# The output projection of a two-branch decoder layer: 512 columns of weights per matmul in place of 256, products in another order

## The chip, the cores and the metric

The kernel runs on one core of a Trainium2 chip. The metric is the device time of one execution in microseconds; the number quoted for a kernel is the median of several runs. The profile is one execution, recorded instruction by instruction, and its span is the time from the first to the last instruction.

## The reference

The layer computes, for a sequence of 512 rows and a model width of 1024 in fp32:

```python
h = rms_norm(x, norm_w)
proj = h @ w_in                       # all queries, keys, values and gates at once
y_a = moba(...) * silu(z_a)           # block-sparse attention, 8 heads
y_b = nsa(...) * silu(z_b)            # compressed + selected + window attention, 8 heads
merged = sigmoid(g_a) * (y_a @ w_branch_a) + sigmoid(g_b) * (y_b @ w_branch_b)
out = x + merged @ w_out              # [512 x 1024] @ [1024 x 1024]
```

The change touches the last line alone: the product with `w_out` and the addition of `x`.

## The kernel before, in words

All large products are made in split precision. An fp32 operand becomes a rounded high part and a remainder, and `mm3` (L373 to L387) multiplies with three matmuls: high by high, low by high, high by low. The stationary operand of the output projection is a 128x128 piece of `merged` (tiles `m`, `mh`, `ml`), and the moving operand is a row of weights.

The product with `w_out` is made from seven half-size products in place of eight. The two matrices are cut into quarters; sums of quarters are multiplied, and the results are added to or taken from the quarters of the output. The sums of `merged` are made by `m_sums` (L1600) on VectorE and ScalarE while the stage before it ends. The sums of weights are made in DRAM by `sum_weights` (L565), which copies one quarter into the buffer `wsum` and adds another quarter by a DMA that accumulates; the GpSimd queue issues the last of these at 406.16 us. `operand(p_, w, j)` (L559) says which DRAM piece product `p_` reads: 1, 2 and 4 read plain quarters of `w_out`, 5, 6, 3 and 7 read sums.

The weights come through one stream, `W` (L316 to L371), a list of tiles in the order of their use. A tile of 128x512 fp32 (256 KB) is loaded by the SP queue into one of six raw buffers (`wr`, L328). Then ScalarE or GpSimd rounds it (`wh`, L350 and L354) and VectorE takes the remainder (`wl`, L359), after which the raw buffer is free for the tile six places on. There are eight buffers for `wh` and eight for `wl`. `W.split` is called to keep the conversion up to four tiles ahead of the matmuls.

The whole program is written out by a planner: it keeps an estimated clock for each engine, and an instruction goes into an engine's stream when the estimate lets it start. Each engine then runs its stream strictly in order, and semaphores hold an instruction until its inputs are there. So a wait in the streams of VectorE, ScalarE or SP also holds all that is queued behind it.

`last` (L1619) writes the output projection. Before the change it works on 256 columns at a time. A tile of weights holds two of the four 128-row slices of a quarter, each 256 columns wide. The order is product 1 and then product 2 for both column halves, then products 5, 6, 3, 7, 4 for the first half, then the same five for the second. For each product and half, two blocks of 128 output rows (`t` is 0 and 1) are made one after the other, each by 12 matmuls of 256 columns into one PSUM bank. After each of these 28 results, `add` (L1638) lets VectorE add a quarter of it, with its sign, to the residual tile `xr` (L1641). The matmuls of a later product go on into the same PSUM accumulator, so they wait for the add before them. When an output block of 128x256 is complete, the SP queue stores it. The four tiles of `x` for the right half (`xr`, 128x512 each) are loaded at the start of `last`, on the same SP queue.

In all the stage issues 7 products x 2 halves x 2 blocks x 4 slices x 3 = 336 matmuls of 256 columns, with 28 weight tiles. The stage before it makes the gated merge (`pbr` and `pgw` are its PSUM tiles), and its last matmul is followed at once by the first of `last`.

## Time and profile before

| what | value |
|---|---|
| three runs | 458.43, 459.62, 459.7 us; median 459.62 us |
| span of the profiled execution | 458.3 us; its own time is not listed apart, the shortest run is 0.1 us above the span |
| TensorE busy (PE) | 450.0 us, 98% of the span |
| VectorE, ScalarE, GpSimd busy | 382.1, 299.7 and 203.8 us |
| first matmul of the output projection | 413.07 us |
| its last matmul starts | 454.51 us |
| last instruction of VectorE starts | 454.83 us |

PE is the matmul part of TensorE and PEld its load of the stationary operand, which runs beside the matmuls. In the trace a matmul is shown from its start until its result is out, and the next one starts before that; so the time that one costs in a stream is the distance from start to start, and not the duration in the row. SPq is the DMA queue of SyncE.

### The profile page before, as it was taken

The page shows a single profiled execution, that of the slowest core. Times are in us where ns is not written, and L with a number is a line of the kernel's source. Part 1 is how long each engine was busy: PE and PEld are TensorE (multiplying, and loading weights), DVE is VectorE, ACT ScalarE, POOL GpSimd, SP SyncE. Part 2 cuts the span into 40 slices and gives each one's busy share as a digit, 9 for nine tenths or more (in the row PEclk, how much of TensorE's full clock was granted, in tenths as well). Part 3 has the DMA queues.
Part 4 walks back from the last instruction along what each step waited for, and adds up shares of the span by engine and source line. Part 5 has one row for each costly group of instructions (what it writes and reads, how often), then busy time and mean ns, then how long its engine had stood idle before and what let it go on. Part 6 is the DMA issues. An engine that isn't in the chain of part 4 may idle for free.

```text
span 458.3 us, 8879 instructions
## 1 busy us (share of the span) xinstructions
PE 450.0 (98%) x2935; PEld 406.5 (89%) x2935; DVE 382.1 (83%) x951; ACT 299.7 (65%) x705; POOL 203.8 (44%) x243
## 2 busy tenths in 40 slices
PE   9999999999999999999999999999999999999996
PEld 7888888899778898889999999989988999999996
DVE  6987799889997787878899899878957699898862
ACT  6865668767978797467786777669654256445420
POOL 1263337865774572276776454655741211210020
PEclk9999999999999999999999999999999999999999
DMA  8876646887965869769978967975866888878862
GB/s 275 280 249 208 210 141 211 195 231 189 261 180 159 226 212 281 249 150 271 250 188 205 243 152 189 272 170 123 254 158 180 238 235 249 233 217 309 263 198 69
DMA packets 55230, 98.23 MB, mean 214 GB/s; under 512 B 5328, under 2 KB 10064, under 8 KB 55184
## 3 DMA queue, kind: packets, MB, share of 16 engines
q1 hardware_dynamic: 39952, 68.30, 46.5%
q0 software_dynamic: 7616, 14.68, 19.6%
q10 hardware_dynamic: 7616, 14.68, 9.5%
q8 instruction: 23, 0.38, 0.3%
q14 instruction: 23, 0.19, 0.1%
HBM read 90.69 MB, written 36.31 MB: 277 GB/s over the span
## 4 chain that ended last, share of the span: by engine, by line
PE 73%; DVE 13%; DMA 5%; ACT 5%; issue 3%; SPq 0%; POOL 0%; DVEq 0%; ACTq 0%; POOLq 0%
PE pgw L384 17%; PE pgt L384 14%; PE pbr L384 10%; PE pgc L384 7%; PE pgf L652 5%; PE O L1082 5%; PE pt L1048 4%; PE po L384 4%; PE sps L1001 2%; PE sps L1002 2%; DVE wl L359 2%; DMA wr<-wsum 2%; DMA T<-rtab 1%; DMA wr<-in_w 1%; DVE sb L1020 1%
## 5 line engine op out<-in xcount | busy, mean ns | idle before, releaser
L359 DVE TENSOR_TENSOR wl<-wr,wh 128x512 fp32r<-128x512 f32 (+1 forms) x150 | 102.6, 696 | 4.7 <-ACT wh L350 2.8
L350 ACT CAST wh<-wr 128x512 fp32r<-128x512 f32 (+1 forms) x125 | 74.1, 608 | 19.3 <-DMA wr<-wsum 11.3
L354 POOL TENSOR_SCALAR wh<-wr 128x512 fp32r<-128x512 f32 (+1 forms) x44 | 33.4, 770 | 115.6 <-DVE wl L359 30.6
L1039 POOL TENSOR_SCALAR P<-P,sst,gate 128x512 f32<-128x512 f32 (+3 forms) x56 | 46.5, 832 | 40.0 <-DVE sst L1038 30.1
L1035 ACT ACTIVATE P<-sb,sst 128x512 f32<-128x512 f32 (+3 forms) x88 | 50.7, 577 | 17.4 <-DVE sst L1020 16.1
L1020 DVE CUSTOM_DVE_ANT_0 sb<-sps,T 128x512 f32<-128x512 f32 (+3 forms) x96 | 45.9, 482 | 15.4 <-PE sps L1002 13.3
L384 PE MATMUL pgt<-wl,hh 128*128 128x512 f32 (+2 forms) x160 | 56.2, 351 | 0.8 <-DVE wl L359 0.8
L384 PE MATMUL pgt<-wh,hh 128*128 128x512 f32 (+2 forms) x160 | 56.9, 355 | 0.0
L384 PE MATMUL pgt<-wh,hl 128*128 128x512 f32 (+2 forms) x160 | 56.2, 351 | 0.0
L384 PE MATMUL pgw<-th,wh 128*128 128x256 f32 x240 | 50.4, 285 | 0.3 <-DVE gm L1493 0.3
L1060 ACT CAST ph<-pt 128x512 fp32r<-128x512 f32 (+2 forms) x72 | 33.8, 476 | 20.8 <-PE pt L1048 19.6
L384 PE MATMUL pgw<-hh,wh 128*128 128x256 f32 x160 | 45.7, 285 | 0.1
L384 PE MATMUL pgw<-hh,wl 128*128 128x256 f32 x160 | 45.0, 281 | 0.0
L384 PE MATMUL pgw<-hl,wh 128*128 128x256 f32 x160 | 44.8, 280 | 0.0
L384 PEld LDWEIGHTS pgw<-th,wh 128*128 128x128 f32 x240 | 40.0, 190 | 1.0 <-DVE gm L1493 0.7
L1048 PE MATMUL pt<-cst,P 128*128 128x128 f32 x232 | 40.7, 273 | 0.2 <-DVE pl L1062 0.2
L1062 DVE TENSOR_TENSOR pl<-pt,ph 128x512 fp32r<-128x512 f32 (+2 forms) x72 | 38.7, 548 | 1.8 <-ACT ph L1060 1.6
L427 POOL TENSOR_TENSOR nr<-nss,mhalf 128x8 f32<-128x8 f32 (+1 forms) x16 | 27.2, 1697 | 21.2 <-DVE nss L426 17.8
L384 PEld LDWEIGHTS pgt<-wl,hh 128*128 128x128 f32 x160 | 30.0, 188 | 5.5 <-DVE wl L359 1.2
L384 PE MATMUL pgw<-th,wl 128*128 128x256 f32 x120 | 33.9, 282 | 0.0
L384 PEld LDWEIGHTS pgt<-wh,hh 128*128 128x128 f32 x160 | 30.1, 188 | 3.8 <-ACT nraw L695 0.2
L384 PEld LDWEIGHTS pgt<-wh,hl 128*128 128x128 f32 x160 | 30.1, 188 | 3.7
(267 smaller groups left out, 1346.1 us busy)
## 6 DMA issues: line engine op xcount, KB each, us to landing
wr<-wsum SPq DMA_DIRECT2D x56, 256.0 KB, 4.3
wr<-in_wtok SPq DMA_DIRECT2D x36, 256.0 KB, 4.5
wsum<-in_wgate ACTq DMA_DIRECT2D x16, 512.0 KB, 4.9
wsum<-wsum POOLq DMA_DIRECT2D x14, 512.0 KB, 6.9
wr<-in_wgate SPq DMA_DIRECT2D x24, 256.0 KB, 4.7
xsum<-th SPq DMA_DIRECT2D x16, 256.0 KB, 2.1
T<-rtab SPq DMA_DIRECT2D x16, 256.0 KB, 5.3
wr<-in_w SPq DMA_DIRECT2D x16, 256.0 KB, 4.3
```

What stands on the lines that cost most here:

```text
L350: e.copy(hi, raw)
L354: e.tensor_scalar(hi, raw, 1.0, 1.0, op0=ALU.mult, op1=ALU.mult)
L359: c.do({"D": cd(n)} if lead else either(n), lambda e, hi=hi, lo=lo, raw=raw: e.tensor_sub(lo, raw, hi.bitcast(F32))).mark((w, 1, i))
L384: nc.tensor.matmul(dst, sts[i][a], mvs[i][b], start=(start and i == a == b == 0), stop=(stop and i == n - 1 and b == 1), skip_group_check= ...
L427: c.do({"p": 430 + POWC * w}, lambda e: e.tensor_tensor(v(dst), v(ss), mhalf[:parts, :w], op=ALU.pow))
L652: nc.tensor.matmul(ps[t][:, :n], (hl if a else hh)[:, k, t * P:(t + 1) * P], w[b], start=(k == a == b == 0), stop=(k == KT - 1 and b == 1))
L1020: e.tensor_tensor_reduce(z["sb"][:, :L], sps[:, :L], T[:, S - L:], scale=-1.0, scalar=3e38, op0=ALU.add, op1=ALU.min, accum_out=st[:, 0, b ...
L1035: e.activation(pv(), z["sb"][:, :L], AF.Exp, bias=st[:, 0, b:b + 1], scale=-1.0, accum_out=st[:, 1, b:b + 1])
L1039: c.do({"P": 315 + 0.834 * L}, lambda e: e.tensor_scalar(pv(), pv(), st[:, 2, b:b + 1], g, op0=ALU.mult, op1=ALU.mult))
L1048: nc.tensor.transpose(pt[:, (b - kb) * P:(b - kb + 1) * P], u.p0 if u.p0 is not None and b == 0 else u.pb[:, POFF[b] + kb * P:POFF[b] + (k ...
L1060: e.copy(z["w"][0], pt[:, :w])
L1062: ch.do({"D": cd(w)}, lambda e: e.tensor_sub(z["w"][1], pt[:, :w], z["w"][0].bitcast(F32)), pt)
```

## The change

The stage keeps its seven products, its 28 tiles of weights and its three matmuls per slice, but:

- A tile of weights holds one 128-row slice of a quarter, 512 columns wide (the host's layout `wo` changes, and with it what lies in the four tiles of each sum).
- A matmul streams 512 columns. For each slice the three matmuls are made for block 0 and then for block 1, each in its own PSUM bank, so a tile serves 6 matmuls of 512 columns where it served 12 of 256.
- The products come in the order 1, 2, 6, 5, 7, 3, 4, each for all columns.
- Product 4, the last, is made slice by slice for block 0 at full width, then for block 1 in two column halves (24 matmuls of 256 columns), the second half in a fresh PSUM bank. The part of product 7 that the second half needs is added by an extra VectorE instruction.
- The adds are 128x512, with three of 128x256 at the end, 16 in place of 28. The stores are seven of 128x512 and two of 128x256 in place of 16 of 128x256.
- The loads of `x` for the right half stand between the slices of product 2 in place of the start of `last`.

So 13 groups of 12 matmuls of 512 columns (156) and 24 matmuls of 256 columns take the place of 336.

The core of the diff:

```diff
@@ -590,8 +590,8 @@
         for p_ in (5, 6, 3, 7):
             tiles.append((operand(p_, 1, j), 512))
         tiles += [(wbr[j, 1], 512), (operand(4, 1, j), 512), (wbr[j + 4, 1], 512)]
-    for p_, c in [(p_, c) for p_ in (1, 2) for c in range(2)] + [(p_, c) for c in range(2) for p_ in (5, 6, 3, 7, 4)]:
-        tiles += [(operand(p_, 2, 2 * c + i), 512) for i in range(2)]
+    for p_ in (1, 2, 6, 5, 7, 3, 4):
+        tiles += [(operand(p_, 2, k), 512) for k in range(4)]
     from_att = set()
     for n_ in ORDER_T:
         if n_ in tlay and tlay[n_][1] == KT:
@@ -1617,10 +1617,6 @@
             mt[n_ + 1, k] = hi, lo, (c, d)[n_ // 2], 256 * (n_ % 2)
 
     def last(ms, xr):
-        for t in range(NT):
-            xr[t, 1] = att("xr", F32)
-            dma(xr[t, 1], x[t * P:(t + 1) * P, 512:], 2048)
-
         def st(p_, t):
             if p_ in (1, 2, 3):
                 r, k0 = {1: (0, 0), 2: (0, 4), 3: (2, 4)}[p_]
@@ -1633,33 +1629,55 @@
                 r.append((hi[:, z], lo[:, z], ch))
             return r
         ps, rd = {}, {}
-        tags = {("a", 0): "ss", ("a", 1): "tt", ("b", 0): "to", ("c", 0): "to", ("b", 1): "gg", ("c", 1): "gg"}
-
-        def add(c, z_, t, r, half, end=False, free=False):
-            xv = xr[r, half][:, c * 256:(c + 1) * 256]
-            src = ps[z_, c, t]
-            ch = Chain(now[0] + 230).do({"D": 335}, lambda e: e.scalar_tensor_tensor(
-                xv, src[:, :256], -0.25 if half else 0.25, xv, op0=ALU.mult, op1=ALU.add), src if free else None)
+        tags = {"a": "ss", "c": "tt", "b": "to"}
+        H = slice(0, 256), slice(256, 512)
+
+        def add(z_, t, r, half, end, free, z):
+            xv, n = xr[r, half][:, z], z.stop - z.start
+            src = ps[z_, t]
+            ch = Chain(now[0] + 230).do({"D": cd(n)}, lambda e: e.scalar_tensor_tensor(
+                xv, src[:, z], -0.25 if half else 0.25, xv, op0=ALU.mult, op1=ALU.add), src if free else None)
             if end:
-                ch.call(lambda: dma(out[r * P:(r + 1) * P, (c + 2 * half) * 256:(c + 2 * half + 1) * 256], xv, 1024))
+                ch.call(lambda: dma(out[r * P:(r + 1) * P, 512 * half + z.start:512 * half + z.stop], xv, 4 * n))
             return ch
-        rest = ((5, "b", True), (6, "a", False), (3, "b", False), (7, "a", False), (4, "a", False))
-        for c, p_, z_, first in ([(c, *z) for z in ((1, "a", True), (2, "c", True)) for c in range(2)] +
-                                 [(c, *z) for c in range(2) for z in rest]):
-            ws = W.take(2, 256)
-            for t in range(2):
-                if first:
-                    tag = tags[z_, c][t]
-                    yield room(tag)
-                    ps[z_, c, t] = psum(tag, "po")
-                elif (z_, c, t) in rd:
-                    yield rd[z_, c, t].ready
-                yield from mm3(ps[z_, c, t][:, :256], st(p_, t), ws, start=first, again=not first)
-                W.split(W.i + 4 + 2 * t)
-                r, half, end, free = {1: (t, 0, False, False), 5: (t + 2, 1, False, False), 6: (t + 2, 0, False, False),
-                                      3: (t + 2, 0, True, True), 7: (t + 2, 1, True, False), 2: (t, 0, True, True),
-                                      4: (t, 1, True, True)}[p_]
-                rd[z_, c, t] = add(c, z_, t, r, half, end, free)
+        def out_of(p_, t):
+            return {1: (t, 0, False, False), 5: (t + 2, 1, False, False), 6: (t + 2, 0, False, False), 3: (t + 2, 0, True, True),
+                    7: (t + 2, 1, True, False), 2: (t, 0, True, True), 4: (t, 1, True, True)}[p_]
+
+        def part(dst, p_, t, k, w, z, start, again):
+            yield from mm3(dst[:, z], [st(p_, t)[k]], [(w[0][:, z], w[1][:, z], w[2])], start=start and not k, stop=(k == 3),
+                           again=again)
+            W.split(W.i + 4)
+
+        full = slice(0, 512)
+        for p_, z_, first in ((1, "a", True), (2, "c", True), (6, "a", False), (5, "b", True), (7, "a", False), (3, "b", False)):
+            for k in range(4):
+                if p_ == 2:
+                    xr[k, 1] = att("xr", F32)
+                    dma(xr[k, 1], x[k * P:(k + 1) * P, 512:], 2048)
+                w = W.take(1, 512)[0]
+                for t in range(2):
+                    if not k:
+                        if first:
+                            yield room(tags[z_][t])
+                            ps[z_, t] = psum(tags[z_][t], "po")
+                        else:
+                            yield rd[z_, t].ready
+                    yield from part(ps[z_, t], p_, t, k, w, full, first, not first)
+                    if k == 3:
+                        rd[z_, t] = add(z_, t, *out_of(p_, t), full)
+                        if (p_, t) == (7, 1):
+                            add(z_, t, t, 1, False, False, H[1])
+        ws = W.take(4, 512)
+        for t, z_, z in ((0, "a", full), (1, "a", H[0]), (1, "d", H[1])):
+            if z_ == "d":
+                yield room("g")
+                ps[z_, t] = psum("g", "po")
+            else:
+                yield rd[z_, t].ready
+            for k in range(4):
+                yield from part(ps[z_, t], 4, t, k, ws[k], z, z_ == "d", z_ == "a")
+            add(z_, t, *out_of(4, t), z)
 
     def cmp():
         yield from compress_h(0)
@@ -1753,7 +1771,7 @@
     w2 = np.stack([f[k][0].reshape(2, P, DH).transpose(1, 0, 2) for k in ("cmp_w2_k", "cmp_w2_v")], 1)
     wbr = np.stack([np.concatenate([ch(f[k][0][:, j * P:(j + 1) * P]) for k in ("w_branch_a", "w_branch_b")], 0)
                     for j in range(8)])
-    wo = f["w_out"][0].reshape(2, 2, 2, P, 2, 2, 256).transpose(4, 0, 5, 1, 3, 2, 6).reshape(4, 4, P, 512)
+    wo = f["w_out"][0].reshape(2, 4, P, 2, 512).transpose(3, 0, 1, 2, 4).reshape(4, 4, P, 512)
     onehot, cd = _consts()
     cd.update(pos=posT.reshape(P, -1), w2=w2.reshape(P, -1))
     d = dict(x=f["x"][0], xT=f["x"][0].T[P:],
```

The planner's streams are the same up to the stage's start; from there they move. The first place is the SP queue behind the loads of the sixth and seventh weight tile of the stage (`wr_6001`, `wr_6014`; the tiles are counted from 0). `wr` are raw weight tiles, `xr` the residual, `wsum` the buffer of summed weights. Before:

```order
L253 DMA wr_6001<-in_wout 128x512
L253 DMA wr_6014<-in_wout 128x512
L253 DMA xr_6030<-in_x 128x512
L253 DMA xr_6032<-in_x 128x512
L253 DMA xr_6034<-in_x 128x512
L253 DMA xr_6036<-in_x 128x512
L253 DMA wr_6064<-wsum_151 128x512
L253 DMA wr_6089<-wsum_151 128x512
L253 DMA wr_6135<-wsum_151 128x512
L253 DMA wr_6164<-wsum_151 128x512
L253 DMA out_y<-xr_5991 128x256 x2
```

The same place after the change:

```order
L253 DMA wr_6001<-in_wout 128x512
L253 DMA wr_6014<-in_wout 128x512
L253 DMA wr_6048<-wsum_151 128x512
L253 DMA wr_6063<-wsum_151 128x512
L253 DMA wr_6071<-wsum_151 128x512
L253 DMA xr_6087<-in_x 128x512
L253 DMA xr_6104<-in_x 128x512
L253 DMA xr_6118<-in_x 128x512
L253 DMA wr_6122<-wsum_151 128x512
L253 DMA wr_6128<-wsum_151 128x512
L253 DMA wr_6137<-wsum_151 128x512
```

The first three loads of summed weights (tiles 8, 9 and 10) moved ahead of the loads of `x`; before, all four loads of `x` stood ahead of tile 8.

The second place is VectorE during the first two products. `gm`, `ma`, `mb`, `ml` belong to the merge and its sums, `wl` is the remainder of a weight tile, and `xr<-po` is an add. Before:

```order
L1573 TENSOR_TENSOR gm_4686<-gm_4686,gm_5813 128x512
L1641 SCALAR_TENSOR_TENSOR xr_5991<-po_6038,xr_5991 128x256
L359 TENSOR_TENSOR wl_6056<-wr_5943,wh_6055 128x512
L1329 TENSOR_TENSOR ma_6024<-gm_4685 128x256
L1641 SCALAR_TENSOR_TENSOR xr_5991<-po_6059,xr_5991 128x256
L1577 TENSOR_TENSOR ml_6023<-gm_4686,mh_6022 128x512
L1330 TENSOR_TENSOR ma_6024<-gm_4686,ma_6024 128x256
L1641 SCALAR_TENSOR_TENSOR xr_5991<-po_6084,xr_5991 128x256
L1332 TENSOR_TENSOR mb_6025<-gm_4686,gm_4685 128x256
L1344 TENSOR_TENSOR ml_6027<-ma_6024,mh_6026 128x256
L359 TENSOR_TENSOR wl_6058<-wr_5965,wh_6057 128x512
L1333 TENSOR_TENSOR mb_6025<-ma_6024,gm_4686 128x256
```

After (the row `gm_4686` stands ahead of these too, and `wl_6037`, `wl_6052` are tiles 4 and 5, `wl_6067` is tile 6):

```order
L359 TENSOR_TENSOR wl_6037<-wr_5943,wh_6036 128x512
L359 TENSOR_TENSOR wl_6052<-wr_5965,wh_6051 128x512
L1329 TENSOR_TENSOR ma_6024<-gm_4685 128x256
L1577 TENSOR_TENSOR ml_6023<-gm_4686,mh_6022 128x512
L1330 TENSOR_TENSOR ma_6024<-gm_4686,ma_6024 128x256
L1332 TENSOR_TENSOR mb_6025<-gm_4686,gm_4685 128x256
L1638 SCALAR_TENSOR_TENSOR xr_5991<-po_6030,xr_5991 128x512
L1333 TENSOR_TENSOR mb_6025<-ma_6024,gm_4686 128x256
L1638 SCALAR_TENSOR_TENSOR xr_5991<-po_6038,xr_5991 128x512
L1341 SCALAR_TENSOR_TENSOR ml_6027<-ma_6024,mh_6026 128x256
L1344 TENSOR_TENSOR ml_6029<-mb_6025,mh_6028 128x512
L359 TENSOR_TENSOR wl_6067<-wr_6001,wh_6066 128x512
```

The remainders of tiles 4 and 5 moved ahead of the merge's sums. Two adds of 512 columns stand where four of 256 stood, and the remainder of tile 6 stands behind both of them and behind the last of the sums. One piece of the sums (`ml_6027<-ma_6024,mh_6026`, 128x256) moved from VectorE to GpSimd, ahead of the rounding of tile 6 (`wh_6066`). That is the only rounding left to GpSimd in the stage; it had six there, and ScalarE does the other five now.

## The prediction

> **What bounds the kernel now.** I read the page first: its span, the busy time of the engines, the clock, and the chain that ended last.
>
> ```profile
> span 458.3 us, 8879 instructions
> PE 450.0 (98%) x2935; PEld 406.5 (89%) x2935; DVE 382.1 (83%) x951; ACT 299.7 (65%) x705; POOL 203.8 (44%) x243
> PEclk9999999999999999999999999999999999999999
> PE 73%; DVE 13%; DMA 5%; ACT 5%; issue 3%; SPq 0%; POOL 0%; DVEq 0%; ACTq 0%; POOLq 0%
> ```
>
> TensorE sets the time, at its full clock from end to end. The stage at issue is the last, so what it saves on TensorE should come off the end one for one, if its supply holds. Next the instructions of the tile `po` by shape, in one view:
>
> ```profile
> L384 PE MATMUL po<-wh,mh x88: 278/283/355, 413.8 to 454.3; 128*128 128x256 f32 x88
> L384 PE MATMUL po<-wh,ml x88: 279/283/283, 413.9 to 454.4; 128*128 128x256 f32 x88
> L384 PE MATMUL po<-wl,mh x88: 279/283/387, 414.0 to 454.5; 128*128 128x256 f32 x88
> L384 PE MATMUL po<-wh,m x48: 278/283/283, 413.1 to 447.9; 128*128 128x256 f32 x48
> L384 PE MATMUL po<-wl,m x24: 283/283/283, 413.3 to 448.0; 128*128 128x256 f32 x24
> ```
>
> These are 88+88+88+48+24 = 336 matmuls. Their 283 ns are not what one costs, since they overlap; the distance between starts is, and the timeline of PE gives it. Its rows for the stage's start, its two breaks and its end (start, duration, what):
>
> ```profile
> 413.07 0.40 PE L384 MATMUL po<-wh,m 128*128 128x256 f32 x2
> ...
> 422.55 0.28 PE L384 MATMUL po<-wh,ml 128*128 128x256 f32 x1
> 422.99 0.39 PE L384 MATMUL po<-wl,mh 128*128 128x256 f32 x1 [0.16 <-DVE wl L359]
> 423.21 0.28 PE L384 MATMUL po<-wh,mh 128*128 128x256 f32 x1
> ...
> 436.41 0.28 PE L384 MATMUL po<-wl,mh 128*128 128x256 f32 x1
> 437.29 0.35 PE L384 MATMUL po<-wh,mh 128*128 128x256 f32 x1 [0.61 <-DVE xr L1641]
> 437.49 0.28 PE L384 MATMUL po<-wh,ml 128*128 128x256 f32 x1
> ...
> 453.31 0.28 PE L384 MATMUL po<-wh,ml 128*128 128x256 f32 x1
> ...
> 454.51 0.28 PE L384 MATMUL po<-wl,mh 128*128 128x256 f32 x1
> ```
>
> From 453.31 to 454.51 lie ten distances: 0.120 us each. At that pace 335 distances make 40.20 us; from 413.07 to 454.51 it took 41.44. The missing 1.24 us are the two breaks: 0.44 and 0.22 where 0.12 each was due (0.42 lost), 0.88 and 0.20 (0.84 lost), 1.26 together. So the stage costs 336 x 0.120 + 1.26 = 41.58 us, nearly all of it matmuls one behind the other.
>
> **The change: the matmuls.** Removed are 336 x 0.120 = 40.32 us. Added are 156 matmuls of 512 columns and 24 of 256. No `po` row has 512 columns, so I look for the nearest rows on PE that do:
>
> ```profile
> 7.62 1.09 PE L652 MATMUL pgf<-wl,hh 128*128 128x512 f32 x4
> ...
> 16.95 1.09 PE L652 MATMUL pgf<-wh,hh 128*128 128x512 f32 x4
> ...
> 410.33 0.40 PE L384 MATMUL pbr<-yh,wh 128*128 128x512 f32 x1
> ```
>
> The first product of the kernel (`pgf`) goes from 7.62 to 16.95 in ten groups of four: 9.33/40 = 0.2333 us. The twelve `pbr` just ahead of the stage go from 410.33 to 413.07: 0.2283. I take 0.2333: there, as in the new stage, the weights are streamed and the PSUM bank changes between matmuls. In `pbr` the weights stand still and one bank is filled. The new stage is then 156 x 0.2333 + 24 x 0.120 = 36.39 + 2.88 = 39.27 us, a gain of 1.05 us on the matmuls (1.83 with the pace of `pbr`; none if 512 columns cost 2 x 0.120). A tile of weights now serves 6 x 0.2333 = 1.40 us.
>
> A rule speaks for less. The Trainium skill, TensorE: Matmul & The Clock Gate, section Wait — 56ns, not 53.3ns?, gives a warm matmul a fixed part of only about 2.5 ns beside its columns. By that, 156 fixed parts fewer would be an estimate of 0.39 us in place of 1.05. The rows here disagree: two halves cost 240 ns and the whole 228 to 233, so a fixed part of 7 to 12 ns goes with each.
>
> **The breaks.** Both are late weights. The first, 422.55, is the remainder of a tile of sums. The chain of waits and the list of DMA issues tell the second, and why loads were slow (first row: start, length; others: count, size, median us from issue to landing; then the total wait of the SP queue, times, longest):
>
> ```profile
> 429.18 6.12 DMA wr<-wsum
> ...
> wr<-wsum SPq DMA_DIRECT2D x56, 256.0 KB, 4.3
> xr<-in_x SPq DMA_DIRECT2D x8, 256.0 KB, 8.2
> out_y<-xr SPq DMA_DIRECT2D x16, 128.0 KB, 2.2
> SPq L253 <- DVE xr L1641: 19.9, 15, 6.4
> ```
>
> A load took 6.12 us from 429.18, and its tile stopped PE at 436.41. The loads of `x` took twice as long as a tile's, and in the SP queue the stage's stores waited 19.9 us for adds, each holding the loads behind it. What the change does to this, from the SP queue's own timeline before:
>
> ```profile
> 408.31 2.50 SPq L253 DMA_DIRECT2D wr<-in_wout  x2
> 410.90 4.05 SPq L253 DMA_DIRECT2D xr<-in_x  x4
> 415.45 4.38 SPq L253 DMA_DIRECT2D wr<-wsum  x4
> ```
>
> Tile 8, the first of sums, was issued at 415.45 behind four loads of `x`. Its raw buffer is free once VectorE has taken the remainder of tile 2, which ran at 411.31 (row below), so now it goes at about 412.0, 3.4 us sooner. Two stores (product 2) stand among the loads of tiles where ten did; the others follow the last tile. They wait for adds that PE lets start near 423.8 and 424.5, and hold the load of tile 16 to about 425.6. Needed is tile 16 at 413.07 + 16 x 1.40 = 435.5, less 1.3 us to round it and take its remainder: 8.6 us for a landing that took 4.3 in the median. So neither break should come back. I count 1.26 us gained, with 0 as the other end.
>
> **VectorE.** It sums less: 28 adds become 13 wide and 3 narrow. What counts is the queue in front of tile 6, where the merge's sums and two wide adds stand. Its rows (timeline, then groups of the last stage with count, busy us and mean ns):
>
> ```profile
> 411.31 0.68 DVE L359 TENSOR_TENSOR wl<-wr,wh 128x512 fp32r<-128x512 f32 x1
> 414.55 0.68 DVE L1573 TENSOR_TENSOR gm<-gm,gm 128x512 f32<-128x512 f32 x1
> 418.78 0.68 DVE L359 TENSOR_TENSOR wl<-wr,wh 128x512 fp32r<-128x512 f32 x1
> 419.38 0.41 DVE L1333 TENSOR_TENSOR mb<-ma,gm 128x256 f32<-128x256 f32 x1
> ...
> L1641 DVE SCALAR_TENSOR_TENSOR xr<-po,xr 128x256 f32<-128x256 f32 x28 | 11.7, 419 | 9.6 <-PE po L384 9.6
> L1519 DVE SCALAR_TENSOR_TENSOR gm<-gm,pbr 128x512 f32<-128x512 f32 x1 | 0.7, 689 | 0.7 <-PE pbr L384 0.7
> L1332 DVE TENSOR_TENSOR mb<-gm,gm 128x256 f32<-128x256 f32 x1 | 0.5, 494 | 0.0
> ```
>
> An instruction of 0.68 us lets the next start after 0.60 (418.78 to 419.38). A wide add is no row; the nearest is L1519, also 512 columns out of PSUM, 0.69. From 414.55: L1573, two remainders (0.60 each), 0.34 + 0.60 + 0.34 + 0.41 for the sums, add, 0.34, add, 0.34, 0.60, and the remainder of tile 6. That is 0.60 x 3 + 1.69 = 418.04 for the first add, which PE releases at 413.07 + 20 x 0.2333 + 0.40 + 0.05 = 418.2. From there 0.61 + 0.34 + 0.61 + 0.34 + 0.60 = 420.7, and 421.4 when the remainder is out. PE asks for it at the third matmul of tile 6, 413.07 + 38 x 0.2333 = 421.9. It holds by 0.5 us. Without the overlaps (0.08 on each of 12) it would be late by 0.4; I take 0 and keep 0.4. Each later tile has more room: tile 8's remainder is out 1.2 us later, and PE wants it 2.8 us later. Behind these, an add waiting for PE holds the remainder of a tile that is needed three tiles on. So with no cost I count the wide adds, GpSimd's sum and ScalarE's five more roundings (0.62 us each, in an engine 65% busy).
>
> **The end.** After the last matmul at 454.51 came:
>
> ```profile
> 454.83 0.42 DVE L1641 SCALAR_TENSOR_TENSOR xr<-po,xr 128x256 f32<-128x256 f32 x1 [1.01 <-PE po L384]
> ```
>
> then a store of 128 KB and the end at 458.3. The same add, store and size stand last after the change, because product 4's second block is cut in halves; nothing gained or lost.
>
> **The sum.** 41.58 - 39.27 = 2.31 us: 1.05 from the matmuls, 1.26 from the breaks. The profiled execution goes from a span of 458.3 to 456.0. The shortest run (458.43) lies 0.1 us above that span, the median (459.62) 1.3 us, so I take the difference off the median: **457.3 us**, 0.5% less. A measurement of this kernel can tell about 0.3% from no change, 1.4 us.
>
> **The rivals.** *One term only.* The matmuls gain nothing (512 columns at 0.240, for 39.27 + 1.05), or a tile stops PE again. For the first: 0.120 stands unmoved over the whole stage, and could be a pace of the data and not of the instruction. Against it: all 512-column rows are under 0.234. Either gives -1.05 to -1.26, so 458.4 to 458.6: no change within 0.3%. Chance 0.23.
>
> *The tiles come too late.* Place: the loop of six raw buffers. A buffer lands some time after its issue, is rounded (0.62) and read (0.68), and must be back in 6 x 1.40 = 8.4 us. The tiles of `xr` show how long a landing can be at the start of this stage (loads and stores together):
>
> ```profile
> DMA to landing us min/median/max: 1.9/3.8/8.8
> ```
>
> It decides from landings of 7.1 us; at 4.3 it holds, at 6.12 barely. With 8.8, if the loads of `x` between tiles 10 and 11 and the wide stores do that, the loop takes 10.1 us, 1.68 per tile: 0.28 late on each of the 20 tiles from 8 on is 5.6, less the 2.1 us that tile 8 is early, +3.5 on 457.3: 460.8, at the upper edge of no change. For it speaks the 8.2 us of `xr`; against it that those came where loads stood densest, and that the change takes loads out of that stretch. Chance 0.05.
>
> *The clock drops.* The granted clock falls once in the trace, after the last matmul (window, PE, PEld, DVE, ACT and POOL busy, then the mean clock):
>
> ```profile
> 457.00:458.40 1.40, 0.00 (x0) 0.00 (x0) 0.00 (x0) 0.00 (x0) 0.00 (x0) 0.67 0.00 0
> ```
>
> Should PE, with a bank change at every third matmul, idle often enough for that, the place would be the stage itself. At half the clock a matmul takes 0.23 us more; a quarter of the 156 would cost 39 x 0.23 = +9.0 us on 457.3, 466.3: slower by 1.5%. It decides from about 16 such matmuls (3.7 us) on. The Trainium skill, TensorE: Matmul & The Clock Gate, section A second HAM failure mode: psum-queue depth-cycling, tells of such a case at 512 columns, where PE idled a little between groups. The trace speaks against it: `pgf` changes banks at every matmul and keeps 0.2333, and PEclk reads 9 in every slice, the breaks' too. Chance 0.02.
>
> **How the numbers follow.** My forecast has 0.70. Within it the pace of `pbr` would give -3.1 us, 456.5; runs of one kernel differ by 1.2 us. So the range begins 0.8 below that, at 455.7. Above it takes in the first rival and half of that spread: 459.2. Of the two others, 0.07 together, the late tiles end at the edge and count as slower. Some runs of the forecast will fall within 0.3%, and some of the first rival's beyond it; they about cancel: faster 0.70, same 0.23, slower 0.07.
>
> **What would show it.** Right: `po` rows of 512 columns with starts 0.228 to 0.234 apart, no row of PE in the stage with an idle time over 0.2 us, the last matmul 38.4 to 39.3 us after the first, tile 8 issued near 412. Wrong: a break near 421.9 (VectorE's queue), a break after 435 with a DMA of `wr` ahead of it in the chain of waits, starts 0.24 apart, or a granted clock under 9.

## The result, and the profile after

The kernel after the change takes 456.23 us in the median of four runs (455.94 to 456.8), the kernel before 459.34 us in the runs beside it. The ratio is 0.9942, with a 95% interval of 0.9926 to 0.9958. The profiled execution took 456.11 us. The page of the kernel after:

```profile
span 454.3 us, 8535 instructions
PE 446.8 (98%) x2779; PEld 397.5 (87%) x2779; DVE 383.5 (84%) x938; ACT 301.8 (66%) x710; POOL 201.4 (44%) x239
PEclk9999999999999999999999999999999999999999
PE 85%; DVE 8%; ACT 4%; issue 2%; POOL 0%; DVEq 0%; ACTq 0%; POOLq 0%
```

TensorE still sets the time. In the chain that ended last, the 5% of DMA are gone, and VectorE fell from 13% to 8%. The instructions of `po` by shape:

```profile
L384 PE MATMUL po<-wh,mh x48: 277/389/402, 415.0 to 450.3; 128*128 128x512 f32 x40, 128*128 128x256 f32 x8
L384 PE MATMUL po<-wh,ml x48: 283/389/396, 415.2 to 450.4; 128*128 128x512 f32 x40, 128*128 128x256 f32 x8
L384 PE MATMUL po<-wl,mh x48: 279/389/504, 415.4 to 450.6; 128*128 128x512 f32 x40, 128*128 128x256 f32 x8
L384 PE MATMUL po<-wh,m x24: 389/389/389, 412.3 to 441.9; 128*128 128x512 f32 x24
L384 PE MATMUL po<-wl,m x12: 389/389/389, 412.7 to 442.1; 128*128 128x512 f32 x12
```

These are the 156 wide and 24 narrow matmuls. The timeline of PE gives what they cost (start, duration, what):

```profile
412.26 0.61 PE L384 MATMUL po<-wh,m 128*128 128x512 f32 x2
...
420.65 0.39 PE L384 MATMUL po<-wh,ml 128*128 128x512 f32 x1
420.89 0.50 PE L384 MATMUL po<-wl,mh 128*128 128x512 f32 x1
421.23 0.40 PE L384 MATMUL po<-wh,mh 128*128 128x512 f32 x1
...
429.68 0.39 PE L384 MATMUL po<-wh,ml 128*128 128x512 f32 x1
...
432.40 0.39 PE L384 MATMUL po<-wh,ml 128*128 128x512 f32 x1
...
447.81 0.28 PE L384 MATMUL po<-wh,mh 128*128 128x256 f32 x1
...
450.56 0.28 PE L384 MATMUL po<-wl,mh 128*128 128x256 f32 x1
```

From 429.68 to 432.40 lie twelve distances of wide matmuls: 0.2267 us each, the pace of nearly the whole stage. The 23 narrow ones from 447.81 on keep 0.120. The only loss is around 420.89, where 0.34 us pass and 0.23 were due; with its neighbours product 2 takes 5.62 us where products 5, 7 and 3 take 5.44, so 0.18 are lost. From 412.26 to 450.56 the stage takes 38.30 us; before it took 41.44. So the stage gained 3.14 us, and the medians differ by 3.11.

The spans differ by more, 4.0 us. The other 0.8 us are not the change: the stage began at 412.26 in place of 413.07, and the product `pgt`, in a part of the program that the change does not touch, had already begun 1.0 us earlier (28.57 in place of 29.56).

The supply, from the list of DMA issues after (count, size, median us from issue to landing) and the waits of the SP queue (total, times, longest):

```profile
wr<-wsum SPq DMA_DIRECT2D x56, 256.0 KB, 3.9
xr<-in_x SPq DMA_DIRECT2D x8, 256.0 KB, 6.0
out_y<-xr SPq DMA_DIRECT2D x7, 256.0 KB, 2.0
SPq L253 <- DVE xr L1638: 12.6, 8, 3.8
```

The waits for adds fell from 19.9 to 12.6 us, and the longest from 6.4 to 3.8. The SP queue's timeline after:

```profile
411.20 4.17 SPq L253 DMA_DIRECT2D wr<-wsum  x3
415.46 2.75 SPq L253 DMA_DIRECT2D xr<-in_x  x3
418.31 3.47 SPq L253 DMA_DIRECT2D wr<-wsum  x3
...
422.36 0.84 SPq L253 DMA_DIRECT2D wr<-wsum  x2
423.87 1.07 SPq L253 DMA_DIRECT2D out_y<-xr  x2
425.05 4.68 SPq L253 DMA_DIRECT2D wr<-wsum  x5
```

The first row holds tiles 8 to 10. Tile 8 goes out at 411.20 where it went at 415.45. Tiles 11 to 15 follow among the loads of `x`, then two stores, then tile 16 at 425.05. VectorE ahead of the one loss, and at the end:

```profile
417.22 0.69 DVE L1638 SCALAR_TENSOR_TENSOR xr<-po,xr 128x512 f32<-128x512 f32 x1
417.83 0.86 DVE L1333 TENSOR_TENSOR mb<-ma,gm 128x256 f32<-128x256 f32 x1
418.62 0.68 DVE L1638 SCALAR_TENSOR_TENSOR xr<-po,xr 128x512 f32<-128x512 f32 x1
...
419.55 0.68 DVE L1344 TENSOR_TENSOR ml<-mb,mh 128x512 fp32r<-128x512 f32 x1
420.15 3.08 DVE L359 TENSOR_TENSOR wl<-wr,wh 128x512 fp32r<-128x512 f32 x5
...
450.88 0.42 DVE L1638 SCALAR_TENSOR_TENSOR xr<-po,xr 128x256 f32<-128x256 f32 x1 [1.01 <-PE po L384]
```

The remainder of tile 6 starts at 420.15 behind the two wide adds and the last sum, and is out at 420.83; the matmul that reads it starts at 420.89, and there the time is lost. In e7_hh and e11_w_64 below, whose matmuls ask for this tile 0.25 us later, product 2 loses nothing. The last add starts 0.32 us behind the last matmul, as before.

### The profile page after: what moved, and what is told of

It reads as the page before. It is cut to its first block, busy times and chain, and to the rows that moved or that the text cites. A ratio compares the mean times of both kernels' runs of the same rounds, so it can differ in the third digit from the quotient of the medians.

```text
span 454.3 us, 8535 instructions
## 1 busy us (share of the span) xinstructions
PE 446.8 (98%) x2779; PEld 397.5 (87%) x2779; DVE 383.5 (84%) x938; ACT 301.8 (66%) x710; POOL 201.4 (44%) x239
## 4 chain that ended last, share of the span: by engine, by line
PE 85%; DVE 8%; ACT 4%; issue 2%; POOL 0%; DVEq 0%; ACTq 0%; POOLq 0%
PE pgw L384 20%; PE pgt L384 14%; PE pbr L384 10%; PE po L384 8%; PE pgc L384 7%; PE O L1082 6%; PE pgf L652 5%; PE pt L1048 5%; PE sps L1001 3%; PE sps L1002 3%; DVE wl L359 1%; DVE vl L359 1%; ACT ks L955 1%; DVE sb L1020 1%; PE pq L924 1%
## 5 line engine op out<-in xcount | busy, mean ns | idle before, releaser
L350 ACT CAST wh<-wr 128x512 fp32r<-128x512 f32 (+1 forms) x130 | 77.2, 609 | 15.8 <-PE po L384 4.7
L354 POOL TENSOR_SCALAR wh<-wr 128x512 fp32r<-128x512 f32 (+1 forms) x39 | 30.3, 787 | 80.5 <-DMA wr<-in_wtok 14.4
```

The source lines that it names most:

```text
L350: e.copy(hi, raw)
L354: e.tensor_scalar(hi, raw, 1.0, 1.0, op0=ALU.mult, op1=ALU.mult)
```

## The experiments

The theory on trial: the gain is the sum of two independent terms, the wider matmul and the supply of weights. Its first rival is that one of them made all of it. Totals carry about 0.15% of uncertainty each, 0.7 us; so for terms below that the stage is compared, from its first to its last `po` start in the profiled execution.

### Width alone: e1_halves

The order, loads, adds and stores of after, each wide matmul cut in two:

```diff
-                    yield from part(ps[z_, t], p_, t, k, w, full, first, not first)
+                    for z in H:
+                        yield from part(ps[z_, t], p_, t, k, w, z, first and z is H[0], not first or z is H[1])
...
-                yield from part(ps[z_, t], 4, t, k, ws[k], z, z_ == "d", z_ == "a")
+                for y in (H if z is full else (z,)):
+                    yield from part(ps[z_, t], 4, t, k, ws[k], y, z_ == "d", z_ == "a")
```

> The changed kernel with each matmul of 512 columns cut into two of 256, in the same order of products, tiles, adds, loads and stores: 336 matmuls of 256 columns. Theory of width: the narrow matmul is what costs, 0.120 us from start to start, so the stage's first to last matmul takes 335 x 0.120 = 40.2 us in place of 38.3 in the changed kernel, the time is 1.9 us above the changed kernel (458.1) and about 1.2 us below the kernel before, which had 41.4 with its two breaks. Rival, order alone: the gain is in the order of loads and adds, the breaks and what surrounds them; then the stage stays within 0.5 us of 38.3 and the time at 456.2.

It took 458.24 us, ratio to before 0.9966 (0.9953 to 0.998). First and last row of the stage in its PE timeline:

```profile
412.96 0.40 PE L384 MATMUL po<-wh,m 128*128 128x256 f32 x2
...
453.15 0.28 PE L384 MATMUL po<-wl,mh 128*128 128x256 f32 x1
```

That is 40.19 us for 335 distances, 0.120 each, and no break. So 41.44 - 40.19 = 1.25 us is what the rest of the change gains, and 40.19 - 38.30 = 1.89 us is the width: 156 x (2 x 0.120 - 0.2267) = 2.07, less the 0.18 that after loses in product 2 and e1_halves does not. Both terms exist.

### The stores of before: e2_before_stores_late

The kernel before, with all stores of the stage held until the last weight tile is loaded:

```diff
             if end:
-                ch.call(lambda: dma(out[r * P:(r + 1) * P, (c + 2 * half) * 256:(c + 2 * half + 1) * 256], xv, 1024))
+                late.append(lambda: dma(out[r * P:(r + 1) * P, (c + 2 * half) * 256:(c + 2 * half + 1) * 256], xv, 1024))
+                ch.call(flush)
             return ch
+
+        def flush():
+            while late and W.loaded == len(W.raws):
+                late.pop(0)()
```

> The kernel before, with the stores of the output held back until the last weight tile is loaded, so that no store stands among the loads of tiles in the SP queue. Theory: the second break (0.84 us lost behind 436.4) comes from loads that wait behind stores; it goes, the stage takes 40.6 us, the time falls by 0.8. The first break (0.42 us at 422.55) is late work of VectorE and stays. Rival: the tile was late because loads are slow in the loop of six buffers; the break stays and the time is that of the kernel before.

It took 459.17 us, ratio 0.9983 (0.9968 to 0.9998), and its stage 40.60 us, 0.84 less than before. The break that stays, in its PE timeline:

```profile
421.59 0.28 PE L384 MATMUL po<-wh,ml 128*128 128x256 f32 x1
422.03 0.38 PE L384 MATMUL po<-wl,mh 128*128 128x256 f32 x1 [0.16 <-DVE wl L359]
```

It is the first break, unchanged. The second, which had cost 0.84 us, is gone whole with the stores out of the way of the loads. In before the late tile did not stop PE itself: its remainder (VectorE, 436.12) stood ahead of an add (436.73), and for that add PE waited, as the row at 437.29 says. The edit also changes which instructions stand next to each other in VectorE's stream, so it does not test the queue of loads alone.

### The loads of x: e3_x_early

The kernel after, with the four loads of `x` back at the start of `last`:

```diff
     def last(ms, xr):
+        for t in range(NT):
+            xr[t, 1] = att("xr", F32)
+            dma(xr[t, 1], x[t * P:(t + 1) * P, 512:], 2048)
...
-                if p_ == 2:
-                    xr[k, 1] = att("xr", F32)
-                    dma(xr[k, 1], x[k * P:(k + 1) * P, 512:], 2048)
```

> The changed kernel with the four loads of x for the right half back at the start of the stage, ahead of the first three tiles of sums. Theory of the prediction (the place of these loads matters): tile 8 is issued some 3 us later, the lead over the matmuls is lost and a break of 0.3 to 1.3 us comes back. Rival: the lead of 2 us at tile 8 and 3 at later ones takes it up; no break, 456.2 within 0.3%.

It took 457.47 us, ratio 0.9944 (0.9925 to 0.9962), which the totals cannot tell from after. Its stage took 38.82 us, 0.52 more. Its PE timeline:

```profile
424.48 0.39 PE L384 MATMUL po<-wh,ml 128*128 128x512 f32 x1
425.09 0.50 PE L384 MATMUL po<-wl,mh 128*128 128x512 f32 x1 [0.23 <-DVE wl L359]
```

The matmul at 425.09 is the first that needs the remainder of tile 8. That remainder in the VectorE timeline, and the add ahead of it:

```profile
423.75 0.69 DVE L1642 SCALAR_TENSOR_TENSOR xr<-po,xr 128x512 f32<-128x512 f32 x1 [1.39 <-PE po L384]
424.36 0.68 DVE L359 TENSOR_TENSOR wl<-wr,wh 128x512 fp32r<-128x512 f32 x1
```

The expectation was right in the size of the break and not in its way. Tile 8 was issued at 413.74 in place of 411.20 and landed at 420.88 in place of 418.43, but ScalarE had rounded it by 421.61, and VectorE then stood idle for 1.39 us: the remainder was queued behind an add of product 2 that waited for PE. In after five remainders, tiles 6 to 10, run ahead of these adds. So the new place of the loads is a part of the gain, through the order that VectorE's stream gets with it. That the planner chose this order because it reckons the tile later is likely, and was not tested.

### The order of products: e4_old_order

The kernel after, with the products in the order of before:

```diff
-    for p_ in (1, 2, 6, 5, 7, 3, 4):
+    for p_ in (1, 2, 5, 6, 3, 7, 4):
...
-        for p_, z_, first in ((1, "a", True), (2, "c", True), (6, "a", False), (5, "b", True), (7, "a", False), (3, "b", False)):
+        for p_, z_, first in ((1, "a", True), (2, "c", True), (5, "b", True), (6, "a", False), (3, "b", False), (7, "a", False)):
```

> The changed kernel with the products in the order of before (1, 2, 5, 6, 3, 7, 4). Product 7 and product 4 then follow each other on one accumulator. Theory: product 4 waits for the adds of product 7, of which block 0's is 0.05 us of release, 0.69 us of add and about 0.05 of release late against 0.68 us of block 1's matmuls, so a break of 0.1 to 0.5 us in front of product 4 and a time 0.1 to 0.5 us above the changed kernel. Rival, order is worth nothing: no break, same time. Should order be worth more than that (the two breaks of before come back), the time rises by 1 us or more.

It took 457.15 us, ratio 0.9944 (0.9926 to 0.9961); its stage 38.71 us, 0.41 more than after. Its PE timeline in front of product 4:

```profile
445.06 0.39 PE L384 MATMUL po<-wl,mh 128*128 128x512 f32 x1
445.65 0.47 PE L384 MATMUL po<-wh,mh 128*128 128x512 f32 x1 [0.20 <-DVE xr L1638]
```

Products 7 and 4 go into the same accumulators, so with 7 last but one PE waits for its add. The new order puts product 3 between them.

### The cut at the end: e5_full_tail

The kernel after, with the last block of product 4 at full width, one add and one store:

```diff
-                        if (p_, t) == (7, 1):
-                            add(z_, t, t, 1, False, False, H[1])
...
-        for t, z_, z in ((0, "a", full), (1, "a", H[0]), (1, "d", H[1])):
+        for t, z_, z in ((0, "a", full), (1, "a", full)):
```

> The changed kernel with the last block of product 4 at full width, one accumulator, one add of 128x512 and one store of 256 KB at the end. Matmuls: 12 of 512 columns (12 x 0.227 = 2.72 us) in place of 24 of 256 (2.88), 0.16 us less. After them: the last add takes 0.69 us in place of 0.42 and the last store 2.00 us in place of 1.71, 0.56 us more. Theory (the tail counts): 0.4 us above the changed kernel. Rival (the store's end does not set the program's end): 0.16 us below it or no difference.

It took 456.96 us, ratio 0.996 (0.9945 to 0.9974). The stage is shorter, 38.00 us. The last add in its VectorE timeline:

```profile
450.57 0.69 DVE L1638 SCALAR_TENSOR_TENSOR xr<-po,xr 128x512 f32<-128x512 f32 x1 [2.03 <-PE po L384]
```

From the last matmul's start (450.14) to the end of the span now pass 4.49 us in place of 3.77. Against 0.30 us less up to that start this is a loss of 0.42, as expected: by these two profiled executions the cut pays. The totals cannot tell the two kernels apart.

### The first break of before: e6_before_no_p1_adds

The kernel before, without the four adds of product 1:

```diff
-                rd[z_, c, t] = add(c, z_, t, r, half, end, free)
+                if p_ != 1:
+                    rd[z_, c, t] = add(c, z_, t, r, half, end, free)
```

> The kernel before without the four adds of product 1 (the output's left half lacks that product in its upper rows): VectorE has 4 x 0.34 us less to do ahead of the remainder of tile 7, and nothing else changes for the loads. Theory: the first break (0.42 us lost from 422.55 on) is VectorE's queue; it goes, only the second stays. Rival, as the prediction had it: it is a late load; it stays.

A single run took 458.98 us, with a stage of 40.69. The break at 422.55 is gone, but another of the same size stands at the remainder of tile 9, two tiles further on, in its PE timeline:

```profile
425.02 0.28 PE L384 MATMUL po<-wh,ml 128*128 128x256 f32 x1
425.46 0.38 PE L384 MATMUL po<-wl,mh 128*128 128x256 f32 x1 [0.16 <-DVE wl L359]
```

And the second break shrank to 0.10 us, though no store was taken out of the way of a load.

The matmul that stopped at 422.99 in before is the first to need the remainder of tile 7, a plain tile of `w_out`. That tile had landed at 417.39 and was rounded by 418.74, 3.5 us before its remainder started (422.25); VectorE was busy with the sums, adds and other remainders until then. So the first break is VectorE's queue and no late load. The new break has the same form as the one of e3_x_early: tile 9 was rounded by 421.89, but its remainder (424.72) stood behind two adds for which VectorE sat idle, 0.92 and 0.42 us, until PE was done. So taking four adds away moves the break and does not remove it. In after the remainders of tiles 6 and 7 run one behind the other (420.15 and 420.76), where two adds and a sum stood between them before; that this is what removed the first break fits the rows and was not tested apart.

### Why 0.2267 and not 0.2333: e7_hh and e8_hh_values

`pgf` uses pieces of `hh` and `hl` as its stationary operand, `po` uses `m`, `mh` and `ml`. First `po` gets those of `pgf`:

```diff
         def st(p_, t):
+            return [(hh[:, k, t * P:(t + 1) * P], hl[:, k, t * P:(t + 1) * P], None) for k in range(4)]
```

> The changed kernel with slices of the layer's normalized input (hh, hl) as the stationary operand of the whole stage in place of the merged gates' (so the output is another product). The question is the pace of a matmul of 512 columns: 0.2333 in the first product of the kernel, which has this stationary operand, and 0.227 in the changed kernel's last stage. Theory A, the pace goes with the stationary operand (its place in memory or its values): 0.233 here, the stage's 156 wide matmuls 1.0 us longer. Theory B, it goes with the stage (what the other engines and the DMAs do, or the order of banks): 0.227 as in the changed kernel. The 24 narrow ones at the end: 0.117 by A, 0.120 by B.

A single run took 458.87 us. Two rows of its PE timeline:

```profile
429.64 0.39 PE L384 MATMUL po<-wh,hh 128*128 128x512 f32 x1
...
432.44 0.39 PE L384 MATMUL po<-wh,hh 128*128 128x512 f32 x1
```

Twelve distances make 2.80 us, 0.2333 each; over the whole stage the 156 take 36.40 us, the same. So another stationary operand changes the pace, with the stage, its banks and its moving operand as they were. The matmuls of 256 columns at the end change too:

```profile
450.64 0.28 PE L384 MATMUL po<-wh,hh 128*128 128x256 f32 x1
...
453.32 0.28 PE L384 MATMUL po<-wl,hh 128*128 128x256 f32 x1
```

23 distances make 2.68 us, 0.1167 each: with this operand two narrow matmuls cost no more than a wide one, and the width would gain nothing. Then its values alone, copied to the place of `m`:

```diff
-            ch.do({"A": ca(w_)}, lambda e: e.copy(a[:, :w_], g0[:, :w_]))
-            ch.do(either(w_), lambda e: e.tensor_sub(b[:, :w_], g0[:, :w_], a[:, :w_].bitcast(F32)))
+            ch.do({"A": ca(w_)}, lambda e: e.copy(a[:, :w_], hh[:, j, :w_].bitcast(F32)))
+            ch.do(either(w_), lambda e: e.tensor_add(b[:, :w_], hl[:, j, :w_].bitcast(F32), hl[:, j, :w_].bitcast(F32)))
```

> The changed kernel with the values of hh (high) and of twice hl (low) copied into the tiles that hold the merged gates' high part and remainder, at their own place in memory (so products 1, 2 and 3, which read these tiles, are of other data). If the pace goes with the values of the stationary operand, products 1, 2 and 3 run at 0.233 and the other four at 0.227; if it goes with the operand's place in memory or with the stage, all seven run at 0.227.

A single run took 456.86 us. Product 3, which reads the copied values, from its first row to the first of product 4:

```profile
440.39 0.62 PE L384 MATMUL po<-wh,m 128*128 128x512 f32 x2
...
445.83 0.39 PE L384 MATMUL po<-wh,mh 128*128 128x512 f32 x1
```

24 distances make 5.44 us, 0.2267 as in after, and product 1 takes the same. The values do not matter; what is left is where the operand lies. By the addresses of the built program, `hh` and `hl` start at a multiple of 64 bytes in their partitions, and `wh`, `wl`, `m`, `mh` and `ml` 32 bytes past one.

### Moving hh, or all the others: e9_hh_32 and e10_all_64

An unused tile of 32 bytes (cleared once at the start) ahead of `hh` and one behind `hl`; in the second kernel only the one behind:

```diff
+    gapa = cp.tile([P, 8], F32, name="gapa")
+    nc.gpsimd.memset(gapa, 0.0)
     hh = cp.tile([P, KT, S], F32R, name="hh")
     hl = cp.tile([P, KT, S], F32R, name="hl")
+    gapb = cp.tile([P, 8], F32, name="gapb")
+    nc.gpsimd.memset(gapb, 0.0)
```

> The kernel after with a tile of 32 bytes a partition, written by nothing, ahead of hh and another behind hl: hh and hl then start 32 bytes past a multiple of 64 bytes in each partition, as all the other operands do in the kernel after; nothing else moves against those. Theory of the shared phase: the pace of a product depends on whether its two operands start at the same place within 64 bytes. Products with hh then run like those of the last stage, 226.7 ns at 512 columns in place of 233.3 and 120 ns at 256 columns in place of 116.7; by the counts of the program 528 wide ones save 3.5 us and 576 narrow ones with 96 of 280 columns lose 2.1 us, so 1.4 us less where TensorE sets the time: 454.8 us (454.3 to 456.2). Rival, hh itself (its own region or use): products with hh stay at 233.3 and 116.7 and the time at 456.2.

> The kernel after with one tile of 32 bytes a partition, written by nothing, behind hl: every operand then starts at a multiple of 64 bytes in its partition, hh at the place that it had. Theory of the shared phase: products with hh take 226.7 ns at 512 and 120 ns at 256 columns, as in e9_hh_32, and the last stage keeps 226.7: 454.8 us (454.3 to 456.2). Rival, hh itself: products with hh stay at 233.3 and 116.7, the last stage at 226.7, and the time at 456.2. A second rival, the phase of the moving operand alone (a multiple of 64 gives 233.3): the last stage goes from 226.7 to 233.3, 1.0 us longer, and so does every other product: 457 us or more, and 116.7 in the narrow ones takes some of it back.

The first took 456.27 us, ratio 0.9929 (0.9913 to 0.9944), the second 455.30 us, ratio 0.991 (0.9893 to 0.9928). `pgf` in the PE timeline of e9_hh_32:

```profile
9.33 1.08 PE L656 MATMUL pgf<-wh,hl 128*128 128x512 f32 x4
...
13.90 1.08 PE L656 MATMUL pgf<-wh,hh 128*128 128x512 f32 x4
```

Twenty distances make 4.57 us, and 4.58 in e10_all_64 (8.91 to 13.49): 0.229 in both, where 0.2333 stood. `pgt` went the same way, from 68.78 to 67.84 and 67.81 us for its 288 wide matmuls (all distances summed), and the last stage kept 0.2267 in both. The two rivals fall, since neither kernel left `hh` at its pace, and the last stage did not slow at a multiple of 64. The theory holds in its direction and not in its sizes: half to two thirds of the 6.6 ns went; the narrow matmuls with `hh` did not slow from 117 to 120 ns; and the product `pgc` kept 0.2333, with both operands at the same place within 64 bytes. In the total, e9_hh_32 did not show the 1.4 us.

### The reverse: e11_w_64 and e12_hh_all_64

Last, the place is changed for the weights alone, which should slow the stage at issue, and the slow kernel e7_hh is given equal places. The first edit puts a tile of 32 bytes ahead of the first `wh` and one behind the last `wl`; the second is the one of e10_all_64, made on e7_hh:

```diff
+    def mk(i, n_, tag, ga, gb):
+        if i in from_att:
+            return att(n_)
+        ga and gap(ga)
+        t = wp.tile([P, WT], F32R, name=nm(n_), tag=tag)
+        gb and gap(gb)
+        return t
...
+    W = Stream(tiles, NRAW - 1, lambda i: mk(i, "wh", "whi", "gapa", None), lambda i: mk(i, "wl", "wlo", None, "gapb"))
```

> The kernel after with two tiles of 32 bytes a partition, set to zero once and not used, around the weights' rounded tiles and remainders (wh, wl): these then start at a multiple of 64 bytes, as hh and hl do; the merged tiles (m, mh, ml) stay 32 bytes past one. Nothing else moves against those. Theory of the shared phase: what the first and the fifth product (pgf, pgt) gained in e9_hh_32 they gain here too (233.3 to about 229.5 ns at 512 columns), and the last stage loses it: 226.7 becomes 230 to 233, so its 156 wide products take 0.5 to 1.0 us more, 38.8 to 39.3 us from the first to the last. Rival, the phase does not matter for the last stage and hh alone gained in e9_hh_32 and e10_all_64 for another reason: pgf and pgt as after, 233.3, the last stage 226.7.

A single run took 456.25 us. Its last stage, in its PE timeline:

```profile
429.76 0.40 PE L384 MATMUL po<-wh,mh 128*128 128x512 f32 x1
...
432.56 0.40 PE L384 MATMUL po<-wh,mh 128*128 128x512 f32 x1
```

Twelve distances make 2.80 us: 0.2333. The same tiles, values and order as in after, moved by 32 bytes against each other, lose the whole 6.6 ns: 36.40 us for the 156 in place of 35.55. The narrow ones at the end took 0.118. In the median `pgf` and `pgt` went to 0.231 to 0.232, and `pbr`, whose weights moved too, from 0.228 to 0.232 in its three kinds of rows to 0.233 to 0.234. That the time is not above that of after, in spite of the 0.82 us that the stage lost, goes with the matmuls of 256 columns in `pgw`: all distances of these 840 sum to 100.3 us in place of 102.35.

> The kernel of e7_hh (the last stage takes its stationary operand from hh and hl, so that it computes another product) with one tile of 32 bytes behind hl, as in e10_all_64: all operands at multiples of 64 bytes. In e7_hh the wide products took 233.3 ns. Theory of the shared phase: 229 to 230 here, as in pgf and pgt of e10_all_64, or 226.7 if the phase is all there is to it: the stage 156 x 3.7 to 6.6 ns = 0.6 to 1.0 us shorter than in e7_hh. Rival, the place of hh itself: 233.3 stays.

A single run took 454.42 us. The same stretch of its last stage:

```profile
429.68 0.39 PE L384 MATMUL po<-wh,hh 128*128 128x512 f32 x1
...
432.43 0.39 PE L384 MATMUL po<-wh,hh 128*128 128x512 f32 x1
```

0.2292 on average, and 35.77 us for the 156 where e7_hh had 36.40: 0.63 less, the low end of what was expected. So equal places within 64 bytes are worth about 3 to 7 ns of a wide matmul in four of the five products seen (`pgf`, `pgt`, `pbr`, `po`). What makes up the rest between 0.2267 and 0.229, and why `pgc` does not follow, was not settled. By the addresses of the built programs, `hh` and the weights still lie 64 bytes apart within 128 in e9_hh_32, e10_all_64 and e12_hh_all_64, where `m` and the weights lie alike; whether that is the rest was not tested.

## Why the prediction was right

The result, 456.2 us in the median and 3.1 less than before, lies inside the range, and the gain has the two terms that were forecast. One of them was mis-sized, and the breaks were read wrong in part. Two of its signs of being right were missed by little, 0.2267 where 0.228 was the least and 38.30 where 38.4 was; both go with the pace.

- **TensorE sets the time, and the stage's gain comes off the end.** Right: 3.14 us in the stage, 3.11 in the medians.
- **The matmuls, 1.05 us.** Right in kind, too small: 1.89 us. The step that failed is "I take 0.2333". The other end that was given, the pace of `pbr` with 1.83 us, was the nearer one. The reason given for the choice was wrong: e7_hh and e11_w_64 show that neither streamed weights nor the change of banks set that pace, but where the operands lie. And 1.05 is a difference between two placements: with the operands that give 0.2333 two narrow matmuls take 2 x 0.1167 (e7_hh), and like for like the gain would have been nothing. That it came out with the right sign owes something to luck. The trace of before had the hint: `pgt` with `hh` has 234 ns at 512 columns and 117 at 256 (medians).
- **The page's rule.** The Trainium skill, TensorE: Matmul & The Clock Gate, section Wait — 56ns, not 53.3ns?, gave a fixed part of about 2.5 ns and so an estimate of 0.39 us. The trace of after does not agree: two narrow matmuls cost 240 ns, the wide one 226.7, so 13.3 ns went with each pair. With the operands 32 bytes apart the same difference is 2.7 ns in e11_w_64 and none in e7_hh.
- **The breaks, 1.26 us.** Right in size: 1.25 by e1_halves, with 0.18 lost anew in after. "Both are late weights" holds for the second alone, which goes when the stores are held back (e2_before_stores_late), and there the late tile stopped PE through an add queued behind its remainder. Of the first, the text said that it is "the remainder of a tile of sums". That is wrong: it is tile 7, a plain one, rounded 3.5 us before VectorE came to it. The early loading of tile 8 is no answer to it. It goes with an order on VectorE that avoids a break in the new stage (e3_x_early, 0.52 us); that an add waiting for PE holds a remainder was seen in the text and counted at nothing, which after bears out and e3_x_early does not.
- **Tile 8 near 412.0, tile 16 near 425.6.** Issued at 411.20 and 425.05, in a stage that began 0.81 us earlier. Relative to its start that is exact for the one, 0.26 late for the other; tile 16 landed 5.5 us on, well ahead of its need.
- **VectorE's queue, room of 0.5 us.** Wrong by little and at the place named: a loss of 0.18, with 0.4 given as the other end. The faster pace asked for tile 6 earlier, by 38 x 0.0066 = 0.25 us, and one sum (L1333) took 0.86 us in place of 0.41.
- **The end.** Right: 3.77 us from the last matmul's start, before 3.82.
- **The rivals.** "One term only" falls with e1_halves. "The tiles come too late": tile 8, issued just ahead of the stage, did take 7.2 us, but those issued in the stage at most 5.8, against 7.1 needed in tile after tile. "The clock drops": PEclk reads 9 in every slice.

The time itself is off by 1.1 us: 0.84 of it is the pace (36.39 us forecast for the wide matmuls, 35.55 measured, with the 0.18 inside). The forecast was also taken from a median of 459.62; over more runs before stands at 459.34.

## What to carry to other kernels

Doubling the columns of a matmul saved 13 ns a pair here where both operands start alike, and 0 to 3 ns where they start 32 bytes apart. So take the cost of both widths from operands at the same places, and not only of the same shape. What surrounds the matmuls was worth 1.25 us beside 1.89: look at which stores stand ahead of the tiles in the queue of loads, and which adds that wait for matmuls stand ahead of a tile's conversion. When an accumulator is used again, put another product in between.

## What the runs showed of the hardware

The pace of a matmul of 512 columns depended on where its two operands start within 64 bytes of a partition: 226.7 ns with both alike and 233.3 with 32 bytes between them, for the same tiles in the same stage (after and e11_w_64). The stage was tried at one more place, 64 bytes apart within 128 (e12_hh_all_64, with `hh` as the stationary operand), and took 229.2; so the runs do not show that 64 bytes is the measure. At 256 columns the stage goes the other way: 120 ns in after, 118 in e11_w_64 and 117 in e7_hh. That is no rule: in `pgw` of e11_w_64 the matmuls with `hh`, then alike, went from 118 to 114 in the median, and those with `th`, then apart, from 120 to 117. With `hh` the gain was smaller (229), and one product did not follow. A tile of 32 bytes that aligns all operands (e10_all_64) gives 455.30 us, below both kernels: 0.991 of before, with an interval (0.9893 to 0.9928) that just touches that of after (0.9926 to 0.9958). The two were not run side by side. Beside the 0.97 us in `pgt`, its trace has 0.85 us less in the 480 matmuls of `pgw` with `hh` (57.76 to 56.91 us, all distances summed); why these gained was not tested. Such a sum holds waits too: it is 58.08 in before and 58.39 in e7_hh.
